# Scheduling priorities of ten instruction groups in a streaming encoder layer: mixers and memory layer

## The chip, the cores and the metric

The kernel runs on one core of a Trainium2 chip. The metric is the device time of one execution in microseconds (us). The engines are named as in the profile: PE is TensorE's matmul stream and PEld its weight loads, DVE is VectorE, ACT is ScalarE, POOL is GpSimd, and SP is the engine whose instructions issue the loads and stores of this kernel. A name with a q behind it, such as SPq, is an engine's own instruction queue.

## The reference

One layer is computed for two request groups that share the weights: 2048 prompt frames, and 32 sample frames with caches. The width is 1024, and everything is float32.

```
h = rmsnorm(x, g_pre_mix)
qa, ka, va, qb, kb, vb, g_low, r = split(h @ w_in)        # 512 x3, 256 x2, 512, 16, 512
oa = softmax(qa @ ka.T / 8 + bias(clipped distance)) @ va  # 8 heads x 64, own 64-frame chunk + 8 before it
ob = GLA(qb, kb, vb, log_sigmoid(g_low @ w_alpha2 + b) / 16)  # 4 heads, S_t = diag(a_t) S_(t-1) + k_t^T v_t
x1 = x + rmsnorm(concat(oa, rmsnorm(ob) * g_gla * silu(r)) @ w_o, g_post_mix)
mk, mv = rmsnorm(mem) @ w_mk, rmsnorm(mem) @ w_mv          # 256 memory tokens, 4 heads x 256
x2 = x1 + rmsnorm(softmax(h1 @ w_mq @ mk.T / 16) @ mv @ w_mo, g_post_mem)   # h1 = rmsnorm(x1, g_pre_mem)
y  = x2 + rmsnorm((silu(h2 @ w_gate) * (h2 @ w_up)) @ w_down, g_post_ffn)   # h2 = rmsnorm(x2, g_pre_ffn), hidden 2816
```

The outputs are y for both groups, the attention keys and values, the final GLA states, and the memory keys and values.

## The kernel before

The frames are cut into blocks: `BLK` has three of 512 and one of 544 (the sample's 32 frames ride at the end) for the mixers, and `CB` has five of 416 for the memory layer. Blocks pass from stage to stage through DRAM tiles (`od`, `x1d`, `h1d`, `x2d` and others).

A dense product keeps float32 accuracy by splitting each operand into a high and a low part (`split`: ACT copies the high part, POOL or DVE subtracts). `mm3` (L131) then issues three matmuls for each 128-row slice, at L137, which all dense products share. Their results stand in a ring of two PSUM banks (the tag "dense"), from which an engine copies them.

There are three phases. The **mixers** come first. For a block b, the attention of b is woven with dense work: the input products of the next block, the output product `out_proj` of the block before, or, in the last blocks, the keys and values of the memory (`mem_kv`, tiles `mkps`). The **memory layer** follows (L853 to L1014), and the **FFN** last.

In the mixers' attention, `band_group` takes two 128-frame tiles of two heads at a time. For a head and a tile, one or two score tiles `s` (128 x up to 512) are filled by two matmuls each (`scores`, L437). They lie in a ring of two PSUM banks, "band". `soft_unit` reads them with a DVE instruction that adds the bias and takes the row minimum (L408; in the order listings its kind is ISA, with a second row that reads the minimum into `mn`). ACT applies the exponential (L411), and DVE takes the reciprocal (L412) and scales (L413), which gives the tile `u…_sb`. PE transposes it in pieces of 128 columns, three to a PSUM tile `pt`, of which there is one bank (L492). ACT copies each to `prt` (L493), PE multiplies by the values into the one bank `po` (L442), and DVE's `take` copies that to the output tile (L447).

The GLA mixer (`gla_gates`, `gla_mix`) computes decayed products in PSUM tiles "gla", of which there are two. DVE multiplies the level scores by a mask (L620, `gmask`) and sums over levels (L622). A narrow slice of the input product, `wvr_ps`, is copied to `wvr_st` (L317) and transposed on PE into `wvr_lps` (L321).

`out_proj` computes `wops` tiles by `mm3`. ACT or DVE copies each to `ys` (L736). Its squares are summed on DVE (L719), a matmul with ones (L725, `sqa_ps`) gives the norm, and `resid` multiplies each of the eight 128-row slices of the block on DVE (L745), adds the residual on POOL (L746), and stores it.

In the memory layer, `mem_h` loads `h1d` and splits it, `mem_q`, `mem_attn` and `mem_out` do the products. `mem_out` copies `mops` tiles on DVE, and `mem_fin` loads the residual `xr` (L992), normalises, adds on POOL (L994) and stores (L995).

What sets the order: the kernel is written as a sequence of helpers, and a list scheduler then puts each engine's instructions into a fixed order. An instruction that is ready and has the higher priority goes first, and priority follows the place in the program text. `tc.high_priority(offset=n)` lets the instructions inside it count as n places earlier, and a negative n as later. On the chip each engine runs its list in that order, and semaphores hold an instruction until its inputs and its buffer are free.

Of the kernel before, what the change touches and what calls it, by code (L numbers as in the profile page):

```python
# [2 lines left out]

# [8 lines left out]
ALU = mybir.AluOpType  # L12
# [4 lines left out]
P = 128  # L17
# [28 lines left out]
def encoder_step(ctx, tc, ins, outs):  # L46
    nc = tc.nc
    PE, ACT, DVE, POOL, SP = nc.tensor, nc.scalar, nc.vector, nc.gpsimd, nc.sync
# [24 lines left out]

    flip = [0]
    lo_set = [[nc.gpsimd, nc.vector, nc.gpsimd]]

    def split(hi, lo, src, lo_eng=None):
        ACT.copy(hi, src)  # L78
# [53 lines left out]
    def mm3(ps, parts, first=True, last=True, skip=False):  # L132
        seq = []
        for (lh, ll), (rh, rl) in parts:
            seq += [(lh, rh), (lh, rl), (ll, rh)]
        for i, (a, b) in enumerate(seq):
            PE.matmul(ps, lhsT=a, rhs=b, start=first and i == 0, stop=last and i == len(seq) - 1, skip_group_check=skip)  # L137

    def weave(*lists, lead=1.0):

# [16 lines left out]
    x1d = [dpool.tile([D, n], F32, name=f"x1d{b}") for b, (_, n) in enumerate(BLK)]  # L157
    h1d = [dpool.tile([D, n], F32, name=f"h1d{b}") for b, (_, n) in enumerate(BLK)]
# [20 lines left out]
    with ExitStack() as ph:  # L179
# [176 lines left out]
        gmask = kp.tile([P, 7, 64], F32, name="gmask")  # L356
# [44 lines left out]
        def soft_unit(halves, nb_view, nq, ncol, name):  # L401

            sb = up.tile([P, 640], F32, tag="sb", name=name + "_sb")
            mn = up.tile([P, 4], F32, tag="mn", name=name + "_mn")
            c0 = 0
            for i, ps in enumerate(halves):
                w = ps.shape[1]
                DVE.tensor_tensor_reduce(out=sb[:nq, c0 : c0 + w], in0=ps, in1=nb_view[:, c0 : c0 + w], scale=1.0, scalar=3.0e38 if i == 0 else mn[:nq, 3:4], op0=ALU.add, op1=ALU.min, accum_out=mn[:nq, 0:1] if i == len(halves) - 1 else mn[:nq, 3:4])  # L408
# [25 lines left out]
        def scores(ps_out, qd, ql, ks, e, q0, nq, k0, ncol):  # L434

            for i, q in enumerate((qd, ql)):
                PE.matmul(ps_out, lhsT=q[:, e, q0 : q0 + nq], rhs=ks[:, e, k0 : k0 + ncol], start=i == 0, stop=i == 1)  # L437

        def values(po, v, prt, rows, e, n):

# [138 lines left out]
        def gla_mix(tk, n, st, name, kq, v, laR, sg):  # L579
# [5 lines left out]
            for f in range(2):  # L585
# [18 lines left out]
            for f in range(2):  # L604
                W = Ws[f]
                for e in range(2):
                    h = 2 * f + e
                    rs = slice(e * 64, e * 64 + 64)
                    kf, qf = kq[rs, f, 0], kq[rs, f, 1]
                    ms = gp.tile([P, 7, 64], F32, tag="ms", name=f"{name}_ms{h}")  # L610
                    sps = pm.tile([P, 8, 64], F32, tag="gla", name=f"{name}_s{h}")
                    at = at_p[h]
                    if n == P:
                        PE.matmul(sps[0:64, 7, :], lhsT=W[rs, 1, 0:64], rhs=W[rs, 1, 64:128], start=True, stop=True)
                        for li in range(7):
# [3 lines left out]
                        ACT.copy(at[0:64, 64:128], sps[0:64, 7, :])  # L619
                        DVE.tensor_tensor(out=ms, in0=sps[:, 0:7, :], in1=gmask, op=ALU.mult)  # L620
                        for bk in (slice(0, 64), slice(64, 128)):
                            DVE.tensor_reduce(out=at[bk, bk], in_=ms[bk].rearrange("p a b -> p b a"), axis=AX.X, op=ALU.add)  # L622
# [77 lines left out]
        def out_proj(b):  # L700
            s, n = BLK[b]
            chunks = even_split(n, 512)
            mv, y, ys, accs = {}, [], [], []
# [26 lines left out]
            def tile_m(m):  # L730
                w = load_w(wp, ins["w_o"][0], m * P, P, f"wo{b}_{m}")
                c0 = 0
                for ci, cn in enumerate(chunks):
                    ps = pd.tile([P, 512], F32, tag="dense", name=f"wops{b}_{m}_{ci}")
                    mm3(ps[:, :cn], [(w[k], (mv[k][:, 0, c0 : c0 + cn], mv[k][:, 1, c0 : c0 + cn])) for k in order])
                    (ACT.copy if m % 2 else DVE.tensor_copy)(ys[m][:, c0 : c0 + cn], ps[:, :cn])  # L736
                    c0 += cn
                square(m, "sqa")

# [88 lines left out]
        for b in range(NB):  # L828
# [21 lines left out]


    lo_set[0] = [POOL, DVE]
    with ExitStack() as ph:  # L853
        hp = ph.enter_context(tc.tile_pool(name="bh", bufs=3, **RW))
        kv = ph.enter_context(tc.tile_pool(name="bkv", bufs=1, **RW))
# [26 lines left out]
        def mem_h(b):  # L882
            s, n = CB[b]
            mv = []
            for k in range(KT):
                raw = hp.tile([P, 416], F32, tag="hr", name=f"h1_{b}_{k}")
                for bb, lo, hi, off in pieces(BLK, s, s + n):
                    SP.dma_start(raw[:, off : off + hi - lo], h1d[bb][k * P : (k + 1) * P, lo:hi])
                m_ = (mpa if k < 5 else mpb).tile([P, 2, 416], F32R, tag="mov", name=f"m2_{b}_{k}")
                split(m_[:, 0], m_[:, 1], raw)  # L890
                mv.append(m_)
            return mv
# [77 lines left out]
        def mem_out(b, mo):  # L970
            s, n = CB[b]
            y = []

            def tile_m(m):
                w = load_w(wp, ins["w_mo"][0], m * P, P, f"wmo{b}_{m}")
                ps = pd.tile([P, 512], F32, tag="dense", name=f"mops{b}_{m}")
                mm3(ps[:, :n], [(w[k], (mo[k][:, 0], mo[k][:, 1])) for k in range(KT)])
                yt = xps[b % 2].tile([P, 416], F32, tag="xy", name=f"y2_{b}_{m}")
                DVE.tensor_copy(yt, ps[:, :n])
                y.append(yt)  # L980

            return [partial(tile_m, m) for m in range(KT)] + [partial(mem_fin, b, y)]

        def mem_fin(b, y):
            s, n = CB[b]
            last = b == len(CB) - 1
            with tc.high_priority(offset=2 * PRI if last else 0):
                r = norm_fm(np_, pn, y, n, f"n3_{b}")
                for k in range(KT):
                    xr = np_.tile([P, 416], F32, tag="xr", name=f"xr{b}_{k}")  # L990
                    for bb, lo, hi, off in pieces(BLK, s, s + n):
                        SP.dma_start(xr[:, off : off + hi - lo], x1d[bb][k * P : (k + 1) * P, lo:hi])  # L992
                    DVE.scalar_tensor_tensor(out=y[k], in0=y[k], scalar=gains["g_post_mem"][:, k : k + 1], in1=r, op0=ALU.mult, op1=ALU.mult)
                    (DVE if last and k % 2 else POOL).tensor_tensor(out=y[k], in0=y[k], in1=xr, op=ALU.add)  # L994
                    SP.dma_start(x2d[b][k * P : (k + 1) * P, :], y[k])  # L995
                r = norm_fm(np_, pn, y, n, f"n4_{b}")
                for k in range(KT):
                    DVE.scalar_tensor_tensor(out=y[k], in0=y[k], scalar=gains["g_pre_ffn"][:, k : k + 1], in1=r, op0=ALU.mult, op1=ALU.mult)
                    SP.dma_start(h2d[b][k * P : (k + 1) * P, :], y[k])

        load_kv()
        mv = mem_h(1)
        out = []
        for b in range(len(CB)):
# [6 lines left out]
            out = mem_out(b, mo)  # L1011
# [9 lines left out]
    with ExitStack() as ph:  # L1021
# [116 lines left out]
        for b, (s, n) in enumerate(CF):  # L1138
# [213 lines left out]
```

## Time and profile before

| | |
|---|---|
| median of three runs | 3488.55 us (3488.55 to 3490.67) |
| the profiled execution's own time | 3487.48 us |
| its span | 3485.7 us |
| mean granted PE clock | 0.974 of full speed |
| busy: PE, PEld | 95%, 89% of the span |
| busy: DVE, ACT, POOL | 67%, 48%, 38% |
| mixers, memory layer, FFN | about 0 to 1500, 1450 to 2000, 1990 to 3486 us |

The line numbers in all rows of the profile are those of the kernel before. A row of waits names the engine and tile that waited, the engine, tile and line that released it, the microseconds in total, how often, and the longest. A row of windows gives the stretch, its length, each engine's busy time with its number of instructions, then the granted PE clock, the share of the DMA engines' time, and GB/s.

### The profile page before, as it was taken

The numbers are of one execution on the slowest core, as the hardware profiler recorded it, in microseconds if no ns is written. First come the engines' busy times: TensorE is split into PE (matmuls) and PEld (weight loads), VectorE is DVE, ScalarE is ACT, GpSimd is POOL, SyncE is SP. The second block draws the span as 40 slices with busy tenths as digits, with TensorE's granted clock in tenths as the row PEclk, the third lists the DMA queues.
The fourth block names the chain that finished last, engine by engine and source line by source line (L and its number), as shares of the span: only waits on it lengthen the run. The fifth ranks groups of instructions, "written<-read, shape, count | busy, mean of one in ns | idle before, by whom it ended". The sixth has DMA issues, their size and how long they took to land. (4 is left out here: it accounts for less than half of the span.)

```text
span 3485.7 us, 60212 instructions
## 1 busy us (share of the span) xinstructions
PE 3305.2 (95%) x22211; PEld 3113.8 (89%) x22211; DVE 2351.4 (67%) x4395; ACT 1671.8 (48%) x3733; POOL 1320.4 (38%) x1086
## 2 busy tenths in 40 slices
PE   7999999999998989899999789999899999999998
PEld 6888988989987778789999689999899999899998
DVE  4578687664567887486666685666976657866665
ACT  4455455453455555465555443334543334533334
POOL 3233232132144434344533453333453334533332
PEclk9999999999999989999999899999999999999999
DMA  8865664555446555665645542222242223222222
GB/s 248 261 214 169 188 184 139 165 172 158 125 145 203 173 169 172 200 210 161 187 144 167 172 136 79 73 73 74 94 138 73 79 77 92 93 91 73 73 73 90
DMA packets 550044, 488.56 MB, mean 140 GB/s; under 512 B 48488, under 2 KB 496801, under 8 KB 549749
## 3 DMA queue, kind: packets, MB, share of 16 engines
q1 hardware_dynamic: 549749, 484.71, 45.2%
q8 instruction: 174, 2.85, 0.3%
q14 instruction: 121, 0.99, 0.1%
HBM read 369.68 MB, written 114.91 MB: 139 GB/s over the span
## 5 line engine op out<-in xcount | busy, mean ns | idle before, releaser
L137 PE MATMUL pdn<-u,wd 128*128 128x346 f32 (+1 forms) x3168 | 526.0, 323 | 13.1 <-DVE up L1042 9.8
L137 PEld LDWEIGHTS pdn<-u,wd 128*128 128x128 f32 x3168 | 509.7, 190 | 15.7 <-DVE up L1042 10.4
L78 ACT CAST wg_s<-wg_r 128x512 fp32r<-128x512 f32 x231 | 139.5, 620 | 410.7 <-PE pdn L137 198.6
L137 PE MATMUL pg_X<-mf,wg_s 128*128 128x346 f32 (+1 forms) x1584 | 282.4, 327 | 8.7 <-DVE mf L82 3.1
L1042 DVE TENSOR_TENSOR acc<-acc,pdn 128x346 f32<-128x346 f32 (+1 forms) x464 | 231.1, 510 | 87.2 <-PE pdn L137 87.1
L137 PE MATMUL pu_X<-mf,wu_s 128*128 128x346 f32 (+1 forms) x1584 | 282.2, 323 | 0.0
L137 PEld LDWEIGHTS pg_X<-mf,wg_s 128*128 128x128 f32 x1584 | 259.4, 192 | 12.7 <-ACT mf L78 4.1
L137 PEld LDWEIGHTS pu_X<-mf,wu_s 128*128 128x128 f32 x1584 | 257.9, 190 | 0.4
L82 POOL TENSOR_TENSOR wu_s<-wu_r,wu_s 128x512 fp32r<-128x512 f32 x132 | 176.3, 1336 | 210.2 <-ACT wu_s L78 202.6
L82 POOL TENSOR_TENSOR wg_s<-wg_r,wg_s 128x512 fp32r<-128x512 f32 x99 | 136.0, 1375 | 302.6 <-ACT wg_s L78 291.9
L137 PE MATMUL wops<-om,wo_s 128*128 128x512 f32 (+1 forms) x960 | 209.0, 366 | 16.0 <-ACT om L78 9.3
L137 PE MATMUL wvr_ps<-wvr_s,mv 128*128 128x256 f32 (+3 forms) x1632 | 216.5, 286 | 1.2 <-DVE wvr_s L82 1.2
L82 POOL TENSOR_TENSOR u<-sg,u 128x346 fp32r<-128x346 f32 (+1 forms) x132 | 135.0, 1033 | 198.6 <-ACT u L78 198.6
L137 PE MATMUL mops<-mo,wmo_s 128*128 128x416 f32 x960 | 199.9, 358 | 5.9 <-DVE wmo_s L82 4.4
L137 PEld LDWEIGHTS wvr_ps<-wvr_s,mv 128*128 128x128 f32 (+1 forms) x1632 | 200.6, 183 | 4.7 <-DVE wvr_s L82 1.4
L137 PEld LDWEIGHTS wops<-om,wo_s 128*128 128x128 f32 x960 | 158.4, 196 | 41.6 <-ACT om L78 10.5
L137 PEld LDWEIGHTS mops<-mo,wmo_s 128*128 128x128 f32 x960 | 179.1, 191 | 11.1 <-DVE wmo_s L82 5.4
L78 ACT CAST wu_s<-wu_r 128x512 fp32r<-128x512 f32 x231 | 136.3, 618 | 89.3 <-DVE wu_r L1042 34.0
L137 PE MATMUL mqps<-m,wmq_s 128*128 128x416 f32 x768 | 165.9, 365 | 6.1 <-DVE wmq_s L82 6.1
L442 PE MATMUL po<-prt,v 128*128 128x128 f32 x1120 | 168.4, 281 | 0.8 <-ACT prt L493 0.7
L411 ACT ACTIVATE u_sb<-u_sb,u_mn 128x640 f32<-128x640 f32 (+4 forms) x128 | 97.6, 763 | 120.4 <-DVE u_mn L408 120.0
L442 PEld LDWEIGHTS po<-prt,v 128*128 128x128 f32 x1120 | 150.2, 195 | 5.4 <-ACT prt L493 1.1
(410 smaller groups left out, 7911.0 us busy)
## 6 DMA issues: line engine op xcount, KB each, us to landing
wg_r<-in_w_ffn_gate_dram SPq DMA_DIRECT2D x66, 512.0 KB, 3.7
wu_r<-in_w_ffn_up_dram SPq DMA_DIRECT2D x66, 512.0 KB, 4.0
wd_r<-in_w_ffn_down_dram SPq DMA_DIRECT2D x66, 512.0 KB, 3.5
wmq_r<-in_w_mq_dram SPq DMA_DIRECT2D x80, 256.0 KB, 2.8
wmo_r<-in_w_mo_dram SPq DMA_DIRECT2D x80, 256.0 KB, 2.9
wo_r<-in_w_o_dram SPq DMA_DIRECT2D x64, 256.0 KB, 3.1
ks<-kad SPq DMA_DIRECT2D x28, 512.0 KB, 5.6
wvr_r<-in_w_in_dram SPq DMA_DIRECT2D x48, 256.0 KB, 3.7
```

Of the source, the lines that this page charges most:

```text
L78: ACT.copy(hi, src)
L82: lo_eng.tensor_tensor(out=lo, in0=src, in1=hi.bitcast(F32), op=ALU.subtract)
L137: PE.matmul(ps, lhsT=a, rhs=b, start=first and i == 0, stop=last and i == len(seq) - 1, skip_group_check=skip)
L411: ACT.activation(sbv, sbv, AF.Exp, bias=mn[:nq, 0:1], scale=-1.0, accum_out=mn[:nq, 1:2])
L442: PE.matmul(po[:, e * P : e * P + n], lhsT=v[:kk, j, :], rhs=prt[:kk, j, :n], start=j == 0, stop=j == len(rows) - 1)
L1042: eng.tensor_tensor(out=out, in0=a, in1=b, op=ALU.add)
```

## The change

A helper `led(lead, f, …)` wraps single calls into `high_priority(offset=lead)`. Ten groups get such an offset: in the mixers the dense matmuls of `mm3` (-200, and 0 from the memory layer on), the score matmuls (+3000), `soft_unit`'s DVE add-and-minimum (-3000), GLA's mask product (-600), and the copies of `wops` on ACT and on DVE (+200); in the memory layer the loads of `h1d` (+200), the DVE copies of `mops` (+3000), and the loads of `xr` (+200). The set of instructions is the same, and only their order within the engines' lists differs.

```
+    dense_lead = [-200]
+
+    def led(lead, f, *a, **k):
+
+        with tc.high_priority(offset=lead) if lead else nullcontext():
+            return f(*a, **k)
...
-            PE.matmul(ps, lhsT=a, rhs=b, start=first and i == 0, ...)
+            led(dense_lead[0], PE.matmul, ps, lhsT=a, rhs=b, start=first and i == 0, ...)
...
-                DVE.tensor_tensor_reduce(out=sb[:nq, c0 : c0 + w], in0=ps, ...)
+                led(-3000, DVE.tensor_tensor_reduce, out=sb[:nq, c0 : c0 + w], in0=ps, ...)
...
-                PE.matmul(ps_out, lhsT=q[:, e, q0 : q0 + nq], rhs=ks[:, e, k0 : k0 + ncol], start=i == 0, stop=i == 1)
+                led(3000, PE.matmul, ps_out, lhsT=q[:, e, q0 : q0 + nq], rhs=ks[:, e, k0 : k0 + ncol], start=i == 0, stop=i == 1)
...
-                        DVE.tensor_tensor(out=ms, in0=sps[:, 0:7, :], in1=gmask, op=ALU.mult)
+                        led(-600, DVE.tensor_tensor, out=ms, in0=sps[:, 0:7, :], in1=gmask, op=ALU.mult)
...
-                    (ACT.copy if m % 2 else DVE.tensor_copy)(ys[m][:, c0 : c0 + cn], ps[:, :cn])
+                    led(200, ACT.copy if m % 2 else DVE.tensor_copy, ys[m][:, c0 : c0 + cn], ps[:, :cn])
...
+    dense_lead[0] = 0
...
-                    SP.dma_start(raw[:, off : off + hi - lo], h1d[bb][k * P : (k + 1) * P, lo:hi])
+                    led(200, SP.dma_start, raw[:, off : off + hi - lo], h1d[bb][k * P : (k + 1) * P, lo:hi])
...
-                DVE.tensor_copy(yt, ps[:, :n])
+                led(3000, DVE.tensor_copy, yt, ps[:, :n])
...
-                        SP.dma_start(xr[:, off : off + hi - lo], x1d[bb][k * P : (k + 1) * P, lo:hi])
+                        led(200, SP.dma_start, xr[:, off : off + hi - lo], x1d[bb][k * P : (k + 1) * P, lo:hi])
```

In the listings that follow, a row gives the line, the operation, what it writes and reads, the shape, and how many alike stand in a row. Later lines of the kernel stand six or seven lower in the file with the change, and instructions that pass through `led` carry its line, L81.

**PE, the start of the last block's attention.** `s12_1_0` is the score tile of frame tile 12, head 1, first half; `pt12`, `prt12` and `po12` belong to the same unit; `mkps` and `mkt` are products and transposes of the memory keys, and `wops` the output product of block 0. Before:

```order
L137 MATMUL mkps1_12734<-mm0_3_12649,wmk1_4_s_12731 128x256 x6
L437 MATMUL s13_0_0_13282<-ks12_0_13206,qs12_0_13214 128x320
L437 MATMUL s13_0_0_13282<-ks12_0_13206,ql1_236 128x320
L437 MATMUL s13_0_1_13285<-ks12_0_13206,qs12_0_13214 128x320
L437 MATMUL s13_0_1_13285<-ks12_0_13206,ql1_236 128x320
L492 MATMUL pt12_0_0_13237<-ident_64,u12_0_sb_13229 128x128 x3
L492 MATMUL pt12_0_3_13242<-ident_64,u12_0_sb_13229 128x128 x2
L442 MATMUL po12_0_13222<-prt12_0_13236,v12_0_13207 128x128 x5
L437 MATMUL s13_1_0_13310<-ks12_0_13206,qs12_0_13214 128x320
L437 MATMUL s13_1_0_13310<-ks12_0_13206,ql1_236 128x320
L783 MATMUL mkt1_0_12762<-ident_64,mkf1_12759 128x128
```

With the change, at the place where `mkps1` ends:

```order
L81 MATMUL mkps1_12734<-mm0_2_12640,wmk1_4_s_12731 128x256 x6
L81 MATMUL s14_1_0_13423<-ks14_0_13380,qs14_0_13386 128x320
L81 MATMUL s14_1_0_13423<-ks14_0_13380,ql0_235 128x320
L81 MATMUL mkps1_12734<-mm0_3_12649,wmk1_4_s_12731 128x256
L448 MATMUL po12_0_13222<-prt12_1_13264,v12_0_13207 128x128 x2
L81 MATMUL s14_1_1_13426<-ks14_0_13380,qs14_0_13386 128x320
L81 MATMUL s14_1_1_13426<-ks14_0_13380,ql0_235 128x320
L81 MATMUL mkps1_12734<-mm0_3_12649,wmk1_4_s_12731 128x256 x5
L498 MATMUL pt13_0_0_13296<-ident_64,u13_0_sb_13288 128x128 x3
L498 MATMUL pt13_0_3_13301<-ident_64,u13_0_sb_13288 128x128 x2
L498 MATMUL pt13_1_0_13324<-ident_64,u13_1_sb_13316 128x128 x3
L498 MATMUL pt13_1_3_13329<-ident_64,u13_1_sb_13316 128x128 x2
```

The score tiles of tile 13 stood directly ahead of the transposes of tile 12. They have gone some hundred rows ahead (`s13_1_0` now stands between matmuls of `wops0_0` and `wops0_1`), those of tile 14 stand one pair at a time among the dense matmuls, and what remains together at this place are four groups of transposes for one bank and ten value matmuls.

**DVE, the same place.** The eight rows of L745 (L751 with the change) are the residual step of block 0. Before:

```order
L412 RECIPROCAL u12_0_mn_13230<-u12_0_mn_13230 128x1
L413 TENSOR_SCALAR u12_0_sb_13229<-u12_0_sb_13229,u12_0_mn_13230 128x640
L745 SCALAR_TENSOR_TENSOR y1_0_0_11344<-y1_0_0_11344,g_post_mix_1038,acc1_0_11348 128x512 x2
L745 SCALAR_TENSOR_TENSOR y1_0_1_11345<-y1_0_1_11345,g_post_mix_1038,acc1_0_11348 128x512 x2
L745 SCALAR_TENSOR_TENSOR y1_0_2_11346<-y1_0_2_11346,g_post_mix_1038,acc1_0_11348 128x512 x2
L745 SCALAR_TENSOR_TENSOR y1_0_3_11347<-y1_0_3_11347,g_post_mix_1038,acc1_0_11348 128x512 x2
L412 RECIPROCAL u12_1_mn_13258<-u12_1_mn_13258 128x1
L408 ISA u13_0_sb_13288,u13_0_mn_13289<-s13_0_0_13282,nb12_0_13212 128x320
L408 ISA u13_0_mn_13289 128x1
```

With the change:

```order
L81 ISA u14_0_sb_13401,u14_0_mn_13402<-s14_0_0_13395,nb12_0_13212 128x320
L81 ISA u14_0_mn_13402 128x1
L81 ISA u14_0_sb_13401,u14_0_mn_13402<-s14_0_1_13398,nb12_0_13212,u14_0_mn_13402 128x320
L81 ISA u14_0_mn_13402 128x1
L751 SCALAR_TENSOR_TENSOR y1_0_0_11344<-y1_0_0_11344,g_post_mix_1038,acc1_0_11348 128x512 x2
L751 SCALAR_TENSOR_TENSOR y1_0_1_11345<-y1_0_1_11345,g_post_mix_1038,acc1_0_11348 128x512 x2
L751 SCALAR_TENSOR_TENSOR y1_0_2_11346<-y1_0_2_11346,g_post_mix_1038,acc1_0_11348 128x512 x2
L751 SCALAR_TENSOR_TENSOR y1_0_3_11347<-y1_0_3_11347,g_post_mix_1038,acc1_0_11348 128x512 x2
L418 RECIPROCAL u14_0_mn_13402<-u14_0_mn_13402 128x1
L453 COPY o12_0_13221<-po12_0_13222 64x128 x2
L88 TENSOR_TENSOR wmk3_4_s_12859<-wmk3_4_r_12857,wmk3_4_s_12859 128x512
L81 ISA u14_1_sb_13429,u14_1_mn_13430<-s14_1_0_13423,nb12_0_13212 128x320
```

The first half of `u13_0` stood behind the eight products. With the change both halves of `u13` and of `u14_0` stand ahead of them, and the two copies out of `po12_0` stand behind them.

**PE, the attention of block 2.** `wvr2_1_lps1` is the transpose of the narrow slice that ACT copies from `wvr2_1_ps1` to `wvr2_1_st1`. Before:

```order
L137 MATMUL wvr2_1_ps1_8036<-wvr2_1_6_s_8001,mv2_7_5047 128x272 x3
L206 MATMUL hm1_ps1_8476<-ident_64,hm1_xt_8467 128x128 x4
L437 MATMUL s9_0_0_8767<-ks8_0_8691,qs8_0_8699 128x320
L437 MATMUL s9_0_0_8767<-ks8_0_8691,ql1_236 128x320
L437 MATMUL s9_0_1_8770<-ks8_0_8691,qs8_0_8699 128x320
L437 MATMUL s9_0_1_8770<-ks8_0_8691,ql1_236 128x320
L442 MATMUL po7_3_7338<-prt7_7_7380,v6_3_7266 128x128 x2
L492 MATMUL pt8_0_0_8722<-ident_64,u8_0_sb_8714 128x128 x3
L321 MATMUL wvr2_1_lps1_8064<-ident_64,wvr2_1_st1_8061 16x128
L137 MATMUL wvr2_1_ps2_8067<-wvr2_1_0_s_7986,mv2_0_5012 128x272 x3
```

With the change:

```order
L81 MATMUL wvr2_1_ps1_8036<-wvr2_1_6_s_8001,mv2_7_5047 128x272 x3
L498 MATMUL pt8_0_3_8727<-ident_64,u8_0_sb_8714 128x128 x2
L448 MATMUL po8_0_8707<-prt8_0_8721,v8_0_8692 128x128 x3
L327 MATMUL wvr2_1_lps1_8064<-ident_64,wvr2_1_st1_8061 16x128
L81 MATMUL wvr2_1_ps2_8067<-wvr2_1_0_s_7986,mv2_0_5012 128x272 x3
```

Between the last matmuls into `wvr2_1_ps1` and the transpose of its copy stood thirteen transposes, score and value matmuls. With the change five stand there.

More of the change, by code (lines that the diff above doesn't have):

```diff
@@ L1 @@
-from contextlib import ExitStack
+from contextlib import ExitStack, nullcontext
 from functools import partial
@@ L136, in mm3 @@
         for i, (a, b) in enumerate(seq):
-            PE.matmul(ps, lhsT=a, rhs=b, start=first and i == 0, stop=last and i == len(seq) - 1, skip_group_check=skip)
+            led(dense_lead[0], PE.matmul, ps, lhsT=a, rhs=b, start=first and i == 0, stop=last and i == len(seq) - 1, skip_group_check=skip)
     def weave(*lists, lead=1.0):
@@ L407, in soft_unit @@
                 w = ps.shape[1]
-                DVE.tensor_tensor_reduce(out=sb[:nq, c0 : c0 + w], in0=ps, in1=nb_view[:, c0 : c0 + w], scale=1.0, scalar=3.0e38 if i == 0 else mn[:nq, 3:4], op0=ALU.add, op1=ALU.min, accum_out=mn[:nq, 0:1] if i == len(halves) - 1 else mn[:nq, 3:4])
+                led(-3000, DVE.tensor_tensor_reduce, out=sb[:nq, c0 : c0 + w], in0=ps, in1=nb_view[:, c0 : c0 + w], scale=1.0, scalar=3.0e38 if i == 0 else mn[:nq, 3:4], op0=ALU.add, op1=ALU.min, accum_out=mn[:nq, 0:1] if i == len(halves) - 1 else mn[:nq, 3:4])
                 c0 += w
```

## The prediction

> **What bounds the kernel now.** I read the page first, then a table by stage, then PE's waits in the mixers, then the timelines of PE and DVE around the largest of them, and last the granted clock around the waits.
>
> ```profile
> span 3485.7 us, 60212 instructions
> ...
> PE 3305.2 (95%) x22211; PEld 3113.8 (89%) x22211; DVE 2351.4 (67%) x4395; ACT 1671.8 (48%) x3733; POOL 1320.4 (38%) x1086
> ```
>
> PE is busy for 95% of the span, so the matmuls themselves set the time. A change of order cannot shorten them. It can only take from the 180 us (3485.7 - 3305.2) in which PE stands still, and from the time in which PE runs at a lower clock. The table by stage says where these lie.
>
> ```profile
> 60.00:1040.00 980.00, 955.29 (x7676) 864.36 (x7675) 645.17 (x1548) 504.60 (x1239) 277.57 (x249) 0.99 0.58 178
> 1040.00:1110.00 70.00, 55.15 (x386) 48.18 (x385) 58.62 (x111) 41.67 (x102) 38.12 (x31) 0.90 0.74 233
> 1110.00:1375.00 265.00, 247.35 (x1765) 205.28 (x1763) 210.63 (x452) 142.25 (x376) 101.95 (x86) 0.94 0.53 162
> 1450.00:2110.00 660.00, 608.19 (x3489) 579.54 (x3488) 452.94 (x708) 348.26 (x775) 292.37 (x211) 0.96 0.53 163
> 2110.00:3486.00 1376.00, 1335.11 (x8345) 1323.49 (x8343) 913.48 (x1441) 565.72 (x1090) 549.64 (x437) 0.99 0.27 84
> ```
>
> The second number is the stretch's length and the third PE's busy time. In the mixers from 60 to 1375 us PE is idle for 24.7 + 14.8 + 17.7 = 57.2 us, and from 1040 on the clock is 0.90 and 0.94. From 2110 on it is idle for 40.9 us, but there the order of every engine is the same before and after, so the FFN contributes nothing. In the memory layer the PE order differs by a few swaps only. So the mixers decide. The waits there from 60 to 1375 us (us in total, times, longest):
>
> ```profile
> PE s L437 <- DVE u_mn L408: 11.5, 9, 4.7
> PE pt L492 <- ACT prt L493: 7.5, 8, 1.6
> PE g_o L633 <- DVE at L622: 3.8, 6, 0.8
> PE g_o L631 <- DVE g_ms L620: 2.4, 3, 1.2
> PE wops L137 <- ACT y L736: 1.3, 1, 1.3
> PE wvr_lps L321 <- ACT wvr_st L317: 0.8, 1, 0.8
> ```
>
> The first is a score tile that waits for a bank, which the add-and-minimum of an earlier tile must read out. The second is a group of transposes that waits for the only bank. Both are what the change reorders. The same view for 1040 to 1110 us:
>
> ```profile
> PE pt L492 <- ACT prt L493: 5.2, 5, 1.6
> PE s L437 <- DVE u_mn L408: 4.7, 1, 4.7
> PE mkt L783 <- DVE mkf L779: 2.0, 2, 1.4
> PE g_e L591 <- ACT g_laR L78: 1.8, 1, 1.8
> ```
>
> PE's timeline at that place, then DVE's (start, duration, line; in brackets the idle time before and its releaser):
>
> ```profile
> 1037.10 1.02 PE L725 MATMUL sqa_ps<-acc,ones 128*128 128x512 f32 x2
> 1039.06 3.10 PE L137 MATMUL mkps<-mm,wmk_s 128*128 128x256 f32 x24
> 1044.33 0.44 PE L492 MATMUL pt<-ident,u_sb 128*128 128x128 f32 x2 [1.25 <-ACT prt L493]
> 1044.60 1.34 PE L442 MATMUL po<-prt,v 128*128 128x128 f32 x10
> 1050.66 0.63 PE L437 MATMUL s<-ks,qs 128*128 128x320 f32 x1 [4.72 <-DVE u_mn L408]
> ```
> ```profile
> 1040.69 9.45 DVE L745 SCALAR_TENSOR_TENSOR y<-y,g_post_mix,acc 128x512 f32<-128x512 f32 x8
> 1050.13 0.47 DVE L408 CUSTOM_DVE_ANT_0 u_sb<-s,nb 128x320 f32<-128x320 f32 x1
> ```
>
> PE waits 4.72 us at 1050.66 since the add-and-minimum that frees its bank stands in DVE's list behind eight residual products of 9.45 us.
>
> **The change part by part.** The sum is made against the profiled execution, 3487.5 us (the median of the runs shown is 3488.55, 1.1 above).
>
> *Scores ahead and dense matmuls back, at the start of the last block (1040 to 1110).* The wait of 4.7 goes, because in the new DVE order the reads of `u13` and of `u14_0` stand ahead of the eight products. What is late next are the copies out of `po12_0`, which stand behind them. The eight start 3.6 us after the matmul `sqa_ps` (1040.69 - 1037.10) and take 9.45, so they end 13.0 us after it. The two copies add 0.6 and a reciprocal 0.15: 13.8.
>
> ```profile
> L447 DVE COPY o<-po 64x128 f32<-64x128 f32 x120 | 34.3, 286 | 14.8 <-PE po L442 13.5
> L408 DVE CUSTOM_DVE_ANT_0 u_sb<-s,nb,u_mn 128x320 f32<-128x320 f32 x92 | 50.4, 548 | 7.8 <-PE s L437 4.2
> L317 DVE COPY wvr_st<-wvr_ps 128x272 f32<-128x272 f32 x8 | 3.5, 439 | 3.0 <-PE wvr_ps L137 3.0
> L620 DVE TENSOR_TENSOR g_ms<-g_s,gmask 128x448 f32<-128x448 f32 x64 | 39.6, 620 | 8.4 <-ACT at L619 6.6
> ```
>
> By that time PE has done `sqa`, two transposes, `mkps1` (3.1), five values, four scores and twelve transposes, about 7.1 us at the spacing of the timeline, and has waited three times for the bank of the transposes, which now stand four groups in a row: 3 x 1.25 = 3.75. So it comes to the values of `po13` at 10.9 and waits 13.8 - 10.9 = 2.9. The other waits for `pt` in this stretch are covered, since the order puts 18 to 24 dense matmuls (some 3 us) between the later groups. The sum here: now 5.2 + 4.7 + 2.0 + 1.8 = 13.7, then 3.75 + 2.9 + 3.8 = 10.5, **-3**. Bounds: -7 if the copies are no wait, +3 if the next score tile waits for DVE too.
>
> *The other score waits.* 11.5 - 4.7 = 6.8 us in eight waits. Dense matmuls at -200 are now what PE does when nothing else is ready, so a score that is not ready lets them pass in the schedule. The -3000 on the DVE instruction works the other way: it comes last of all that is ready on DVE, and DVE is busy 210.6 of 265 us. **-4**; bounds -6.8 and +11.5 (as much again as there is now).
>
> *The other waits for `pt`.* 7.5 - 5.2 = 2.3 us: **-1**, bounds -2.3 and +2.3.
>
> *Shorter distances between a copy and its transpose.* With the dense matmuls behind, the ready scores and values are used up earlier, and fewer of them are left to stand between `wvr_ps` and the transpose of its copy: thirteen before and five after in the place shown. Seventeen such transposes exist:
>
> ```profile
> L321 PE MATMUL wvr_lps<-ident,wvr_st x17: 192/272/278, 159.9 to 924.8; 128*16 128x128 f32 x16, 32*16 32x32 f32 x1
> ```
>
> A copy of 0.44 us has no row that gives its whole way from PE over the copy and back; the nearest is the wait for `pt`, 1.25 us behind a copy of about the same length. Five matmuls at 0.134 us (1.34 / 10) cover 0.67 of that, so 0.58 us would show. Seventeen times that are 9.9 us, the upper bound; zero is the lower one, as nearly nothing shows now (0.8). Not all stand so near, and I take half: **+5**.
>
> *The clock.* Windows around the waits, the seventh number being the granted clock:
>
> ```profile
> 1046.00:1056.00 10.00, 4.51 (x18) 3.71 (x18) 9.96 (x18) 2.66 (x6) 4.94 (x4) 0.66 0.69 216
> 1083.00:1090.00 7.00, 4.33 (x18) 3.81 (x19) 6.86 (x15) 2.32 (x8) 2.14 (x2) 0.52 0.93 302
> 1206.00:1213.00 7.00, 7.00 (x63) 6.42 (x63) 6.92 (x21) 1.91 (x6) 0.88 (x1) 0.51 0.70 204
> 1237.00:1250.00 13.00, 11.75 (x35) 8.38 (x36) 8.56 (x26) 4.74 (x13) 3.67 (x3) 0.50 0.71 223
> 1315.00:1322.00 7.00, 7.00 (x38) 5.79 (x35) 6.76 (x10) 0.53 (x4) 0.00 (x0) 0.53 0.21 61
> ```
>
> PE loses its busy time times the missing clock: 1.5, 2.1, 3.4, 5.9 and 3.3, together 16.2 us. Three of these follow waits of the kinds that go (4.72 us at 1050.66, those for `pt`, and, by the next row, a score wait just ahead of the half-speed stretch):
>
> ```profile
> 1239.84 0.64 PE L437 MATMUL s<-ks,qs 128*128 128x320 f32 x1 [1.25 <-DVE u_mn L408]
> ```
>
> They are worth 1.5 + 2.1 + 5.9 = 9.5. I take three quarters, **-7**, because the window at 1206 shows half speed with PE busy throughout, so a wait less need not save the window. Bounds: -16.2, and +7 if as many arise elsewhere. On this the Trainium skill (TensorE: Matmul & The Clock Gate, "Why this matters for your kernels") has a rule: the clock falls after a gap of more than about 3 us between bursts of matmuls. The trace does not bear that out as the only cause, with half speed after 1.25 us and after none. By the rule alone just the 4.72 us wait would have cost clock, this term would be -1.5 and the sum -4.5.
>
> *Terms at nothing.* The mask product at -600 is 64 x 0.62 = 39.6 us of DVE work that PE waits for 2.4 us now (the next step, L622, 3.8); GLA's matmuls have scores and dense work to hide behind, and without that cover it costs up to another 6. The `wops` copies at +200 have one wait of 1.3 us to save and the second bank to hide in: 0, bounds -1.3 and +1.3. In the memory layer PE waits for these above all (1450 to 2110), and the last row is SP's wait to store:
>
> ```profile
> PE pg_Y L137 <- ACT mf L78: 11.2, 1, 11.2
> PE mqps L137 <- DVE wmq_s L82: 6.1, 2, 4.7
> ...
> SPq L995 <- POOL y L994: 28.8, 17, 5.2
> ```
>
> None of PE's is a wait for `h1d`, `mops` copies or `xr`. The `xr` loads pass stores that hold SP's queue for 28.8 us in 17 waits, but each store still waits for POOL, so the weight loads behind it start no earlier; and PE does not wait for `xr`. The `mops` copies may push a split of `wmq` back on DVE. 0, bounds -5 and +5.
>
> Sum: -3 - 4 - 1 + 5 - 7 = -10, so 3487.5 - 10 = **3477.5 us**.
>
> **The rivals.** A difference under 0.2% (7 us) can hardly be told from none.
>
> *Slower: the banks are filled early and read late.* Its place is the two score banks and DVE. The scores go ahead as soon as a bank is free, the read that frees it goes last on DVE, and so at each of the 92 units of two halves (the row of L408) the next one waits a little. At 0.125 us each that is 11.5 us: the score waits double. The copies of the narrow slices cost 0.44 us each in the open (17 x 0.44 = +7.5), and one more half-speed window like 1206 adds 3.4: 3487.5 + 22.4 = 3510. It decides from the point where DVE's other ready work is longer than the PE work between a score tile and the next one on its bank. For it speaks DVE's load of 84% (58.62 of 70) and 79%, and that add-and-minimum instructions alone wait behind 9.45 us in the trace; against it, that the dense matmuls now lie between the scores as cover. Chance 0.33.
>
> *Same: the waits only change places.* The change then does not do what it says. PE's list has the same matmuls, a wait that goes in one ring comes up in the next (as `po13` after `s13`), and the half-speed windows stay. For it speaks that -8 and +5 of my terms nearly cancel without the clock. It gives 3484.5 with the clock unchanged and 3488 where +3.5 more arise. The rule of the skill, by which only the long gap costs clock, gives 3483, which belongs here too. Chance 0.17.
>
> *Faster by much more.* Dense matmuls as general filler halve all idle time from 60 to 1375 (57.2 / 2 = 28.6) and the clock loss (16.2 / 2 = 8.1): 3487.5 - 36.7 = 3451. For it speaks that the dense work is enough to fill everything (the PE is 97% busy from 60 to 1040 with it); against it, that many waits are chains of one unit at a stretch's end, where no dense work is left. Chance 0.15.
>
> **How the numbers follow.** The forecast has 0.35, with a range of its own from 3463 (score and clock terms at 3/2 and more) to 3480.5. Predicted 3477.5. Faster: 0.35 + 0.15 = 0.50; same 0.17; slower 0.33. The range goes down past the large gain to 3448, which leaves out 0.06, and up past the slower case's value to 3512, which leaves out some 0.13.
>
> **What would show it.** In the new trace the wait of 4.7 us for `u_mn` at the start of the last block is gone, and a wait of about 3 us for the copies of `po` stands there instead, with three waits of 1.3 us for `prt` ahead of it. The transposes `wvr_lps` wait for `wvr_st` for some 5 us instead of 0.8. The clock from 1040 to 1375 is over 0.95. The stretches from 1450 on are as long as before within 5 us. I am wrong if the waits of score tiles for `u_mn` from 60 to 1375 are above 11.5 us in total, if the clock in the mixers is no higher, or if the memory layer has changed by over 5 us.

## The result, and the profile after

The changed kernel takes 3490.17 us (median of 12 runs, 3487.15 to 3498.47), the kernel before 3488.75 us (12 runs, 3485.38 to 3493.17). The ratio is 1.0004, with a 95% interval from 0.9995 to 1.0013: no difference that can be told. The range of the prediction holds it; the forecast of -10 us did not come, and the rival "same" did.

The profiled execution of the changed kernel has a span of 3492.5 us, and its time of 3494.23 us is 4 us above the median, so a few microseconds of what follows are that execution's own. First a table by stage, cut at the first query product of the memory layer and the first product of the FFN. Before, from 60 us on (stretch, its length, PE, PEld, DVE, ACT and POOL busy with their instructions, clock, DMA share, GB/s):

```profile
60.00:1481.20 1421.20, 1348.45 (x10428) 1204.83 (x10427) 969.38 (x2195) 738.40 (x1813) 462.73 (x398) 0.97 0.59 180
1481.20:1994.00 512.80, 480.06 (x2677) 455.24 (x2675) 348.60 (x586) 279.09 (x654) 224.40 (x165) 0.96 0.56 174
1994.00:3485.70 1491.70, 1432.04 (x8906) 1416.58 (x8906) 1007.69 (x1551) 623.34 (x1191) 608.56 (x475) 0.98 0.28 88
```

And after:

```profile
60.00:1490.00 1430.00, 1354.20 (x10420) 1205.32 (x10419) 956.63 (x2181) 740.05 (x1809) 462.71 (x398) 0.98 0.58 178
1490.00:2000.10 510.10, 478.36 (x2676) 452.05 (x2674) 349.67 (x585) 280.40 (x654) 233.00 (x165) 0.97 0.56 174
2000.10:3492.50 1492.40, 1436.96 (x8906) 1420.42 (x8906) 1008.33 (x1551) 623.42 (x1191) 608.24 (x475) 0.98 0.28 88
```

The mixers are 8.8 us longer: 5.8 more of PE busy, 3.0 more of PE idle. The memory layer is 2.7 us shorter, and the FFN is alike. That would make two parts of opposite sign, but single executions differ by as much; the experiments below decide it.

PE's groups over the mixers (busy, mean ns, idle time just before them and its releasers), before and then after:

```profile
L442 PE MATMUL po<-prt,v 128*128 128x128 f32 x1120 | 168.4, 281 | 0.8 <-ACT prt L493 0.7
L492 PE MATMUL pt<-ident,u_sb 128*128 128x128 f32 x560 | 102.8, 279 | 7.5 <-ACT prt L493 7.5
L437 PE MATMUL s<-ks,qs 128*128 128x320 f32 (+2 forms) x224 | 80.9, 365 | 14.6 <-DVE u_mn L408 14.6
L321 PE MATMUL wvr_lps<-ident,wvr_st 128*16 128x128 f32 (+1 forms) x17 | 4.6, 268 | 2.6 <-ACT h_xT L207 1.8 <-ACT wvr_st L317 0.8
L783 PE MATMUL mkt<-ident,mkf 128*128 128x128 f32 x16 | 3.7, 321 | 2.0 <-DVE mkf L779 2.0
L137 PE MATMUL mvps<-wmv_s,mm 128*128 128x256 f32 x192 | 31.0, 305 | 0.0
```
```profile
L448 PE MATMUL po<-prt,v 128*128 128x128 f32 x1120 | 177.0, 282 | 12.0 <-DVE o L453 6.5 <-ACT prt L499 5.2 <-issue 0.4
L498 PE MATMUL pt<-ident,u_sb 128*128 128x128 f32 x560 | 105.6, 278 | 3.9 <-ACT prt L499 3.7
L81 PE MATMUL s<-ks,qs 128*128 128x320 f32 (+2 forms) x224 | 81.5, 364 | 7.1 <-DVE u_mn L81 7.1
L327 PE MATMUL wvr_lps<-ident,wvr_st 128*16 128x128 f32 (+1 forms) x17 | 4.6, 269 | 2.2 <-ACT wvr_st L323 1.5 <-DVE wvr_st L323 0.6
L789 PE MATMUL mkt<-ident,mkf 128*128 128x128 f32 x16 | 3.5, 301 | 5.1 <-DVE mkf L785 5.1
L81 PE MATMUL mvps<-wmv_s,mm 128*128 128x256 f32 x192 | 31.1, 311 | 4.0 <-DVE mvf L800 4.0
```

Score waits fall by 7.5 us and waits for `pt` by 3.6. In their place the value matmuls wait 12.0 instead of 0.8, more than half of that for the copies out of `po`, and the transposes of the memory's keys (`mkt`) and the products of its values (`mvps`) wait 9.1 instead of 2.0. At the start of the last block it goes as the prediction's first step says. PE's timeline, then DVE's:

```profile
1050.92 1.02 PE L731 MATMUL sqa_ps<-acc,ones 128*128 128x512 f32 x2
...
1058.09 0.44 PE L498 MATMUL pt<-ident,u_sb 128*128 128x128 f32 x2 [0.76 <-ACT prt L499]
1058.99 0.55 PE L498 MATMUL pt<-ident,u_sb 128*128 128x128 f32 x3 [0.46 <-ACT prt L499]
1060.82 0.44 PE L498 MATMUL pt<-ident,u_sb 128*128 128x128 f32 x2 [1.28 <-ACT prt L499]
1063.91 4.43 PE L448 MATMUL po<-prt,v 128*128 128x128 f32 x20 [2.65 <-DVE o L453]
```
```profile
1053.83 9.46 DVE L751 SCALAR_TENSOR_TENSOR y<-y,g_post_mix,acc 128x512 f32<-128x512 f32 x8 [0.32 <-ACT acc L734]
1063.28 0.57 DVE L453 COPY o<-po 64x128 f32<-64x128 f32 x2
```

The wait of 4.7 us for the score bank is gone. Three waits for the transposes' bank (2.5 us together) and 2.65 us for the copies behind the eight residual products stand there.

### The profile page after: what moved, and what is told of

Its sections match the earlier page's. It is cut to its first block, busy times and chain, and to the rows that moved or that the text cites. A ratio compares the mean times of both kernels' runs of the same rounds, so it can differ in the third digit from the quotient of the medians.

```text
span 3492.5 us, 60178 instructions
## 1 busy us (share of the span) xinstructions
PE 3314.3 (95%) x22211; PEld 3115.0 (89%) x22211; DVE 2346.2 (67%) x4395; ACT 1677.8 (48%) x3733; POOL 1328.7 (38%) x1086
## 5 line engine op out<-in xcount | busy, mean ns | idle before, releaser
L81 PE MATMUL pdn<-u,wd 128*128 128x346 f32 (+1 forms) x3168 | 528.0, 324 | 11.5 <-DVE up L1049 9.8
L81 PEld LDWEIGHTS pdn<-u,wd 128*128 128x128 f32 x3168 | 511.8, 191 | 14.0 <-DVE up L1049 10.4
L81 PE MATMUL pg_X<-mf,wg_s 128*128 128x346 f32 (+1 forms) x1584 | 283.9, 328 | 8.7 <-DVE mf L88 3.3
L81 PE MATMUL pu_X<-mf,wu_s 128*128 128x346 f32 (+1 forms) x1584 | 282.2, 323 | 0.0
L81 PEld LDWEIGHTS pg_X<-mf,wg_s 128*128 128x128 f32 x1584 | 260.8, 193 | 12.6 <-ACT mf L84 4.6
L81 PEld LDWEIGHTS pu_X<-mf,wu_s 128*128 128x128 f32 x1584 | 258.1, 190 | 0.4
L81 PE MATMUL wvr_ps<-wvr_s,mv 128*128 128x256 f32 (+3 forms) x1632 | 222.8, 286 | 1.3 <-DVE wvr_s L88 1.3
L81 PE MATMUL wops<-om,wo_s 128*128 128x512 f32 (+1 forms) x960 | 203.8, 363 | 15.4 <-ACT om L84 14.5
L81 PE MATMUL mops<-mo,wmo_s 128*128 128x416 f32 x960 | 201.8, 360 | 12.1 <-DVE wmo_s L88 8.7
L81 PEld LDWEIGHTS wvr_ps<-wvr_s,mv 128*128 128x128 f32 (+1 forms) x1632 | 202.9, 183 | 6.0 <-DVE wvr_s L88 1.8
L81 PEld LDWEIGHTS mops<-mo,wmo_s 128*128 128x128 f32 x960 | 179.7, 192 | 18.2 <-DVE wmo_s L88 9.5
L81 PEld LDWEIGHTS wops<-om,wo_s 128*128 128x128 f32 x960 | 157.0, 194 | 39.9 <-ACT om L84 15.3
L448 PE MATMUL po<-prt,v 128*128 128x128 f32 x1120 | 177.0, 282 | 12.0 <-DVE o L453 6.5
L81 PE MATMUL mqps<-m,wmq_s 128*128 128x416 f32 x768 | 163.0, 361 | 6.1 <-DVE wmq_s L88 6.1
L81 PEld LDWEIGHTS mqps<-m,wmq_s 128*128 128x128 f32 x768 | 143.0, 191 | 9.9 <-DVE wmq_s L88 7.0
```

The source lines that it names most:

```text
L81: return f(*a, **k)
L448: PE.matmul(po[:, e * P : e * P + n], lhsT=v[:kk, j, :], rhs=prt[:kk, j, :n], start=j == 0, stop=j == len(rows) - 1)
```

## The experiments

Each kernel is the changed one with some of its offsets set to 0 (in one case to 100), and each is compared with the kernel before on the same chip; 0.001 in the ratio is 3.5 us, and brackets hold its 95% interval. The change wraps eight calls, five in the mixers and three in the memory layer; where ten groups are spoken of, these are meant. Some offsets move nothing in the order of any engine when the rest is at 0: those of the mask and the `wops` copies together, and that of the `mops` copies. Setting all to 0 gives the order of before.

**The two halves.** The mixers' five offsets at 0:

```
dense_lead = [0];  led(0, PE.matmul, ps_out, ...);  led(0, DVE.tensor_tensor_reduce, ...)
led(0, DVE.tensor_tensor, out=ms, ...);  led(0, ACT.copy if m % 2 else DVE.tensor_copy, ...)
```

> Only the three offsets of the memory layer (h1d and xr loads, mops copies); the mixers' order is that of before. Theory 1 (the profile after: mixers about 9 us longer, memory layer 2.7 us shorter, FFN alike, so the two parts have opposite signs): the memory layer is 2 to 4 us shorter between its first query product and the FFN's first product, and the whole 3485 to 3487 where before has 3488.7. Theory 2 (the forecast: the memory layer is worth nothing, and the 2.7 us lie within what one execution differs from another): within 1 us of before, 512 to 513 us for the layer.

Measured: 0.9988 [0.9980, 0.9997], about -4 us. Then the other half, with the memory layer's three at 0 (`led(0, SP.dma_start, raw…)`, `led(0, DVE.tensor_copy, yt…)`, `led(0, SP.dma_start, xr…)`):

> Only the five offsets of the mixers; the memory layer's three are at 0. Theory 1: 3492 to 3496, the loss of the mixers shows without the memory layer's gain. Theory 2 (waits only change places, nothing is lost in the mixers): 3487 to 3490. The forecast's own sum for this part was -10, which would be 3479.

Measured: 1.0013 [1.0005, 1.0022], about +4.5 us. The two differences add up to +0.0001, and the change has +0.0004. Theory 1 holds in sign for both, and the memory layer takes 509.2 us in the trace of the first half, 3.6 less than before.

**Which of the memory layer's three.** Only `xr` at +200:

> Only the loads of the residual xr at +200. Its PE order is that of the kernel with all three offsets of the memory layer. Theory 1 (the gain comes through the changed PE order, in which the value products of one block stand a few matmuls later, so that the wait of 5.3 us for their operand goes): a ratio of 0.998 to 0.9997 as with all three, and that wait at 2 us or less. Rival (the loads of h1d or the mops copies give it): 0.9995 to 1.0005 and the wait stays.

Measured: 0.9987 [0.9979, 0.9996]. This load alone gives the gain. PE's waits in the layer, before and with `xr` alone:

```profile
PE mpv L137 <- DVE prR L82: 5.3, 1, 5.3
PE mops L137 <- DVE wmo_s L82: 4.4, 3, 2.9
```
```profile
PE mpv L81 <- DVE prR L88: 1.5, 2, 0.7
PE mops L81 <- DVE wmo_s L88: 6.5, 2, 5.6
```

The layer as a stage with `xr` alone, and ahead of it the mixers of the same execution:

```profile
60.00:1488.50 1428.50, 1354.85 (x10431) 1212.14 (x10431) 969.78 (x2197) 739.54 (x1815) 459.88 (x398) 0.97 0.59 179
1488.50:1996.90 508.40, 477.37 (x2677) 452.00 (x2675) 347.61 (x586) 279.94 (x653) 231.77 (x165) 0.97 0.57 175
```

The wait for `prR` goes, others grow, and the layer takes 508.4 us instead of 512.8, with PE idle 31.0 instead of 32.7. This is not one execution's chance: in the seven kernels here with `xr` at +200 the wait is 1.8 us or less and the layer takes 508.4 to 510.6 us, in the seven without it the wait is 5.3 or 5.4 and the layer takes 512.4 to 520.7. With `xr` earlier the scheduler put the value products `mpv` some matmuls later in PE's list. It also moved instructions in the lists of DVE, ACT, POOL and SP. Which of these moves gives the gain was not tried apart, since one offset makes them all.

**The mixers' offsets apart.** Only the dense matmuls at -200:

> Only the dense matmuls of the mixers at -200. Theory 1 (with dense matmuls last, everything else is cut in between them; PE switches between kinds of matmul more often and its busy time grows, while the waits for score banks shrink): PE busy in the mixers 3 to 6 us above before, waits of score tiles for the add-and-minimum under 8 us instead of 11.5, time 3488 to 3493. Rival (the offset on the scores does that, not the one on the dense matmuls): PE busy and waits as before, 3487 to 3490.

Measured: 1.0004 [0.9993, 1.0015]: nothing that can be told in the time, so neither reading is decided by it. Its score waits are 9.7 us from 60 to 1375, not under 8. Only scores and add-and-minimum:

> Only the score matmuls at +3000 and the add-and-minimum at -3000. Theory 1: about half of the switches and of the loss, 3489 to 3493; score waits under 8 us, since the score tile is filled before the eight residual products. Rival (the slower case of the prediction: filled early and read late): the waits of score tiles rise above 15 us and the time goes to 3495 or more, since the dense matmuls here keep their places and don't cover.

Measured: 1.0041 [1.0027, 1.0054], and in its trace (60 to 1500):

```profile
PE mkt L789 <- DVE mkf L785: 7.7, 4, 4.1
PE po L448 <- DVE o L453: 4.6, 1, 4.6
PE s L81 <- DVE u_mn L81: 1.4, 3, 0.7
```

It is slower, by 14 us, but not as either theory has it: the time is the rival's, yet the score waits nearly vanish, and copies further down the chain are waited for. The prediction's slower case, in which the score banks are read late, thus has the wrong place in this kernel. Only the scores:

> Only the score matmuls at +3000, the add-and-minimum and all else at 0. Theory 1 (the scores ahead are what costs: they use up early the work that later stands beside the chains of the last blocks, so waits come up there in other places): most of the 14 us that scores and add-and-minimum together cost (3493.8 before, 3509.2), thus a ratio of 1.002 to 1.005, with score waits under 4 us. Rival (the late add-and-minimum is what costs): a ratio of 0.999 to 1.001.

Measured: 1.0031 [1.0020, 1.0041], with score waits of 1.9 us. The scores ahead are the cost; without the dense offset the late add-and-minimum adds nothing that can be told. Now beside the dense offset:

> Dense matmuls at -200 and score matmuls at +3000; the add-and-minimum, the mask, the wops copies and the memory layer at 0. With the add-and-minimum at -3000 and the two small ones beside it, the mixers gave 1.0013. Theory 1 (the late add-and-minimum matters little): 1.0005 to 1.002. Rival (it is part of the loss): 0.998 to 1.0003. A third way (it helps, as it keeps other work ahead on DVE): 1.0025 or more.

Measured: 1.0075 [1.0058, 1.0092], the slowest of all. Dense matmuls behind and scores ahead cost 26 us together, and one of the three groups left out must take most of it back (the third way).

> Dense -200, scores +3000 and add-and-minimum -3000; mask, wops copies and memory layer at 0. It stands between dense with scores (1.0075) and all five of the mixers (1.0013). Theory 1 (the late add-and-minimum takes the loss back, since DVE then serves the copies and scalings that PE waits for before it reads scores that are far ahead): 1.0005 to 1.0025. Rival (the mask at -600 and the wops copies take it back): 1.006 to 1.009.

Measured: 1.0025 [1.0016, 1.0034]. The time is in Theory 1's range, but its reason does not show: PE's waits for the copies out of `po` are 8.1 us here against 7.6 without the late add-and-minimum. Putting the add-and-minimum back to -3000 takes off 0.0050, 17 us. The mask and the copies account for at most the step from 1.0025 to 1.0013, whose intervals overlap.

**Versions without the scores ahead.** Dense and memory layer:

> The dense matmuls at -200 and the three of the memory layer; scores, add-and-minimum, mask and wops copies at 0. If the parts add, 1.0004 - 0.0012 gives a ratio of 0.999 (0.998 to 1.0005). Rival (the offsets interact, since the memory layer is scheduled from the state in which the mixers end): 1.000 to 1.002.

Measured: 0.9991 [0.9982, 1.0000]; these two parts add. The changed kernel with only the scores' offset at 0:

```
-                led(3000, PE.matmul, ps_out, lhsT=...)
+                led(0, PE.matmul, ps_out, lhsT=...)
```

> The changed kernel with the score matmuls at 0, the other nine groups as in the change. Theory 1 (the scores' +3000 is the part that costs, the rest of the mixers is worth nothing or a little, the memory layer -0.0012): 0.997 to 0.9995, faster than before and than the change. Rival (late add-and-minimums hurt where the scores are not ahead, since PE then waits for their banks): 1.001 to 1.004, with waits of score tiles over 12 us.

Measured: 0.9952 [0.9941, 0.9964], 3478.1 us where the kernel before took 3494.5 on that chip: faster than both kernels, and by more than Theory 1 has. Its score waits are 11.1 us. And with a small lead of 100:

> The changed kernel with the score matmuls at +100 in place of +3000. Theory 1 (the further ahead, the more it costs): between the kernel without the scores' offset and the change, 0.998 to 1.0. Rival (the place within the order decides, not how far): no relation to these two, 1.0005 or more.

Measured: 1.0049 [1.0036, 1.0061], worse than +3000. The rival holds: the cost does not grow with the lead. Last, with mask and copies at 0 too:

> Dense -200, add-and-minimum -3000 and the memory layer's three; scores, mask and wops copies at 0. It stands between dense with the memory layer (0.9991) and the change without the scores' offset (0.9952). Theory 1 (with the dense matmuls last, the late add-and-minimum is what helps, as it took the loss from 1.0075 to 1.0025 beside the scores): 0.994 to 0.997. Rival (the mask and the wops copies give the difference): 0.998 to 1.0005.

Measured: 0.9945 [0.9931, 0.9959], 3478.0 against 3495.8 us; Theory 1 holds. Beside the dense offset, the late add-and-minimum is worth 0.0046 here (from 0.9991) and 0.0050 with the scores ahead (from 1.0075 to 1.0025). The mask and the copies give nothing that can be told.

So the change consists of these parts: dense matmuls and add-and-minimum behind, about -15 us (0.9945, with the 4 us of `xr` taken off); scores ahead, about +18 (from 0.9952 to 1.0004); the `xr` loads, -4. The traces show where the part of the scores lies. These are rows of the mixers in the kernel with only the scores' offset at 0, to be read against those of the changed kernel:

```profile
L448 PE MATMUL po<-prt,v 128*128 128x128 f32 x1120 | 168.9, 281 | 2.8 <-ACT prt L499 1.5 <-DVE o L453 1.2
L81 PE MATMUL s<-ks,qs 128*128 128x320 f32 (+2 forms) x224 | 79.1, 357 | 11.5 <-DVE u_mn L81 11.1
L789 PE MATMUL mkt<-ident,mkf 128*128 128x128 f32 x16 | 3.6, 310 | 2.8 <-DVE mkf L785 2.8
```
```profile
60.00:1474.10 1414.10, 1347.62 (x10412) 1200.90 (x10411) 958.10 (x2181) 737.69 (x1809) 459.96 (x397) 0.98 0.59 179
```

Without the scores ahead PE waits longer for score banks (11.5 us against 7.1), and before the value matmuls it waits 2.8 us instead of 12.0. The mixers are 15.9 us shorter, of which 9.3 are PE idle (66.5 against 75.8) and 6.6 PE busy. The waits for the copies out of `po` follow the offset through all the traces: they are 2.5 to 10.1 us in the seven kernels with the scores ahead, and at most 1.2 in the seven without.

What lies in PE's busy time can be taken apart. The trace marks the stretches in which the granted clock is half. Half of PE's busy time in them is what the clock costs, by the same rule as in the prediction, and the rest is what the matmuls take at full speed. From the first instruction to the end of the mixers, in us:

| kernel | length | PE idle | cost of the clock | the rest |
|---|---|---|---|---|
| before | 1481.2 | 88.1 | 35.6 | 1357.5 |
| memory layer's three | 1484.2 | 88.2 | 38.5 | 1357.5 |
| `xr` alone | 1488.5 | 89.3 | 42.9 | 1356.2 |
| changed | 1490.0 | 91.0 | 32.7 | 1366.2 |
| mixers' five | 1489.4 | 85.3 | 38.0 | 1366.1 |
| changed, scores at 0 | 1474.1 | 81.0 | 30.2 | 1363.0 |
| dense and scores | 1508.6 | 92.9 | 45.1 | 1370.6 |
| dense, scores, add-and-minimum | 1493.1 | 87.6 | 39.1 | 1366.4 |

The matmuls are the same in all rows, up to one. The first three kernels have one PE order in the mixers, and their last column agrees within 1.3 us, although the clock costs up to 7.3 more in one than in another. The next two have the changed order, agree within 0.1, and stand some 9 us above. So the same matmuls take about 9 us longer in the changed order, with idle time and clock counted out. The ends of matmuls in a profile are modelled, so short pauses between matmuls of different kinds may count as busy there; what these 9 us consist of was not taken apart.

The last two rows differ by the add-and-minimum alone, and its late place takes something off each column: 5.3 us of idle, 6.0 of clock and 4.2 of the rest. Why it helps stays open: it was not tried alone, and no single wait in the traces accounts for 17 us.

## Why the prediction was right, and where its steps failed

**The range held because both signs were in it.** It spans 64 us, from 3448 to 3512. The likeliest case had -10 us, and the case that came had a chance of 0.17. That the time fell into the range is luck as far as the mechanism goes: two large terms, which the last paragraph of this section names, cancelled. None of its three signs of being wrong came either: the score waits from 60 to 1375 fell from 11.5 to 3.9 us, the clock in the mixers is 0.98 instead of 0.97, and the memory layer moved by under 5 us. So these signs could not tell the forecast from its failure.

**"A change of order cannot shorten" the matmuls**: it made them longer. The prediction looked for its gain in PE's idle time and clock alone and put the matmuls' own time as fixed, where the table above has some 9 us more in the new order. Against that, the idle time and the clock moved by +2.9 and -2.9 us in the changed kernel.

**The start of the last block** (-3): the wait of 4.7 went, the copies of `po` cost 2.65 where 2.9 was worked out, the three waits for the transposes' bank 2.5 where 3.75 was. This step is right in mechanism and nearly in size; its sum of -3 for the whole stretch was not measured apart.

**Score waits and `pt`** (-5 beside that): together with the 4.7 us they fell from 22.1 to 11.0 us over the whole mixers, about what the steps say.

**Copies and their transposes** (+5): the place was right and the size was not. The transposes `wvr_lps` wait 2.1 us for `wvr_st` in place of 0.8, and another 1.6 us of the same copies fall on the matmuls `wka_ps`.

**What was missing among the waits**: the copies of `po` away from that one place, `prt` for the value matmuls, and the copies `mkf` and `mvf` of the memory's tiles, some 18 us where 2.8 stood. The prediction asked "what is late next" once, at the largest wait, and took the other waits as going without a successor. The rival "the waits only change places" says just this; PE idle in the mixers moved from 72.8 to 75.8 us.

**The clock** (-7): not shown. In the table the clock costs 35.6, 38.5 and 42.9 us in three executions of the order of before, and 32.7 and 38.0 in two of the changed order, so a term of 7 us lies within what executions of one order differ by. In the changed kernel a half-speed stretch even stands where before had none. The stretch from 470 to 481 us, before and after, then the 3.4 us ahead of it after, and PE's timeline there:

```profile
470.00:481.00 11.00, 11.00 (x138) 9.54 (x137) 10.36 (x20) 5.22 (x15) 4.83 (x4) 1.00 0.68 219
```
```profile
470.00:481.00 11.00, 9.61 (x65) 8.14 (x65) 6.38 (x13) 5.68 (x14) 3.65 (x3) 0.53 0.26 78
467.20:470.60 3.40, 1.46 (x23) 1.06 (x22) 2.39 (x7) 0.18 (x1) 0.98 (x2) 1.00 0.76 246
```
```profile
469.12 0.41 PE L81 MATMUL s<-ks,qs 128*128 128x320 f32 x1 [1.01 <-DVE u_mn L81]
471.39 0.79 PE L448 MATMUL po<-prt,v 128*128 128x128 f32 x2 [1.72 <-ACT prt L499]
```

The clock is 0.53 behind waits of 1.01 and 1.72 us, which begin within 3.4 us in which PE is busy for 1.46. The Trainium skill (TensorE: Matmul & The Clock Gate, "A second HAM failure mode: psum-queue depth-cycling") tells of a kernel whose short idles between groups that cycle through PSUM banks made the clock go back and forth; these rows agree with that better than with the rule of about 3 us in the section "Why this matters for your kernels" of the same page, by which neither wait would matter.

Two readings in this step were wrong besides. The window at 1206 is not half speed "after none": PE waits 2.60 and 0.82 us just ahead of it, in the trace of before:

```profile
1203.74 0.27 PE L614 MATMUL g_s<-g_W 64*64 64x64 f32 x1 [2.60 <-ACT g_W L592]
1205.00 1.40 PE L618 MATMUL g_s<-g_W 64*64 64x64 f32 x18 [0.82 <-DVE g_W L598]
```

And the score wait of 1.25 us at 1239.84 stands inside the half-speed stretch, which begins at 1236.9; the one ahead of it is another score wait, of 1.59 us, at 1235.92.

**The memory layer** (0): wrong by 4 us, within its bounds of 5. The step "PE does not wait for `xr`" is true and beside the point: the offset also changed the lists of all five engines, and a wait of 5.3 us for something else went. The prediction saw the "few swaps" in PE's order and put them at nothing.

**The add-and-minimum at -3000** was counted only as a danger (up to +11.5). Beside the dense offset it is worth -17 us. **The scores at +3000** were counted, with the dense matmuls, as the gain, and are a loss of 18. Two terms of about 17 us, each with the opposite of its forecast sign, cancelled. The prediction followed one ring of buffers at a time, but these offsets change the order of work in all five engines' lists, and the largest effects came up in other places than the rings they were put next to.

## What to carry to other kernels

Price a priority by what it does to the end of the chain, not to the wait that it is put next to: feeding a pipeline earlier at its head cost 18 us here although the waits at the head fell, about half of it since PE then waited at the tail. Try offsets one at a time and then in pairs: alone, dense matmuls behind gave nothing and scores ahead lost 11 us; the pair lost 26, and dense behind with the reader of the scores behind won some 15 (measured with the loads of the memory layer, whose 4 us are taken off). When a change of many parts comes out at zero, switch off its halves first, since here that showed -4 and +4.5 at once, and setting one of the offsets to 0 made a kernel 0.5% faster than both. And do not take the matmuls' own time as fixed: one order took about 9 us more than another for the same matmuls.

## What the runs showed of the hardware

The granted clock makes one order of PE take different times. The kernels with only the dense offset, without and with the memory layer's three, have the same PE order in the mixers:

```profile
60.00:1474.40 1414.40, 1348.68 (x10413) 1200.07 (x10412) 948.93 (x2181) 739.57 (x1809) 461.75 (x397) 0.98 0.59 179
```
```profile
60.00:1489.00 1429.00, 1357.58 (x10417) 1209.27 (x10416) 949.54 (x2181) 739.83 (x1809) 458.18 (x398) 0.97 0.58 178
```

14.6 us lie between them, 8.9 in PE busy and 5.7 in PE idle. Taken apart as in the table above, the clock costs 24.5 and 34.8 us in these windows. So the length of this stage in two single executions shows nothing under some 15 us. The comparisons of many runs tell more, and the last column of the table repeats better (1365.3 and 1362.1 us for these two).

When the clock falls can be read from the fourteen traces together. In all of them every half-speed stretch lasts a multiple of 3.4 us (the cut ends of a trace apart), and all begin on one grid of such steps. From 60 us on, 218 steps at full clock had PE idle for 2.0 us or more in all, and every one was followed by half speed. With 1.7 to 2.0 us idle three in four were, and with under 1.5 us 33 of more than 12,000. It is the sum over the step that goes with the fall, and not one long wait: 175 of the 326 falls had no wait of 3 us or more in the step or reaching into it. Why the clock fell after the 33 is not known.
